# A projection's column blocks in turn: those that VectorE convolves with those that ScalarE copies out

## The chip, the core and the metric

The program runs on one core of one Trainium2 chip. The core has five engines that each work through a list of instructions in order: TensorE (matrix products, PE in the profile), VectorE (DVE), ScalarE (ACT), GpSimd (POOL) and SyncE (SP, which here only starts transfers). Sixteen DMA engines move data between the chip's memory and the core's SBUF. TensorE writes its results into PSUM, in banks, from which VectorE or ScalarE must fetch them. The metric is the device time of one execution in microseconds (us).

## What is computed

One layer of a hybrid decoder, for a prompt of 1,024 tokens and for 8 single new tokens. One input projection feeds three parallel branches; their results are gated, joined and projected back.

```python
h = rms_norm(x) * (1 + scale[:, None]) + shift[:, None]
proj = jnp.dot(h, w['in'])
q_a, k_a, v_a, xbc, dt_raw, qkv_c, beta_raw, a_raw, z = jnp.split(proj, idx, axis=-1)
...
o_a = diff_attention(...)            # q_a, k_a, v_a; the 8 tokens also read a paged cache of 4,096 positions
xbc = jax.nn.silu(causal_conv(xbc) + conv_b)     # Mamba-2 branch, 1,024 columns
qkv = jax.nn.silu(causal_conv(qkv_c))            # gated DeltaNet branch, 3 x 4 heads x 128 columns
... each branch * jax.nn.silu(z)                 # 3 x 512 columns
out = jnp.dot(jnp.concatenate([o_a, o_b, o_c], axis=-1), w['out'])
x = x + gate[:, None] * out
```

## The kernel before, in words

**The projection.** Its columns are done in 44 blocks of 128: 4 of q, 4 of k, 4 of v, 8 of x (the Mamba columns), 12 of z (the gates) and 12 of the DeltaNet branch, three (q, k, v) for each of its heads 0 to 3. `proj_fm` takes the blocks in the order of the list `groups`. A block is three chunks of 344 tokens. A chunk is 24 matmuls (line 458: 8 pieces of the depth, times three products of a split fp32: `whi`*`hh`, `whi`*`hl`, `wlo`*`hh`) into one PSUM bank. The banks come from the ring `pj`, which has three, so a chunk can start only when the chunk three before it has been fetched. After its matmuls a chunk's `sink` runs. A v or z block is fetched by ScalarE, one copy a chunk (lines 600 and 996). An x or DeltaNet block needs a causal convolution over four tokens, which VectorE computes straight out of PSUM: one multiplication (line 969) and three multiply-adds (helper line 167) a chunk, then a copy of the last tokens (line 976, `tail`).

**Silu.** After its third chunk a convolved or z block waits in the list `late_silu`. `silu_flush` gives the list to ScalarE: one activation each, then a load of the table that exp and ln need (line 186), then each block's store to memory. In the kernel before, the list is flushed after three blocks of a DeltaNet head and after two blocks of x or z. ScalarE loads a table (1.28 us) whenever the next function is not in the loaded one; helper line 155 stands for its activations.

**What runs beside.** `drive` interleaves several generators by their costs while the program is written; the framework's scheduler then fixes one order for each engine. Beside the last 33 blocks run: the DeltaNet heads (`gdn_head`, one after another; each needs its three blocks, transposes and scales them, then inverts small triangles by 31 steps on VectorE, tile `U`, with two trips through memory whose transfers ScalarE starts: lines 1129 and 1132 before the steps, 1149 and 1152 after them), the attention of the 8 tokens over the cache (`sample_attention`: a page pair comes in by SP's queue, GpSimd multiplies it, line 840, VectorE reduces it, line 841; after each token's softmax, tile `wz`, TensorE multiplies the value pages, line 896), the weights of the coming blocks (`w_load` on ScalarE's queue, split by ScalarE, tile `whi`, and GpSimd, line 201), and `ssd_sample`, the Mamba step of the 8 tokens (tiles `sst` and `stm` on GpSimd and VectorE). It runs in four quarters, and needs every x block's `tail` (through `conv_sample`) and the z blocks 4 to 7.

**The parts.** `CUTS` splits the 33 blocks into parts. Each part drives its blocks with a share of the heads' and of the pages' work; `ssd_sample` is given to the part that begins after block 18. When the projection ends, the rest (attention of the prompt, the last head, the Mamba scan, the output projection) follows.

The order of the last 33 blocks before is: four v, head 1's three, x 0 to 3, head 2's three, x 4 to 7, twelve z, head 3's three. So from the fifth to the eighteenth VectorE fetches every chunk (called the conv run below), and in the twelve z blocks ScalarE does (the z run).

## Time and profile before

| | us |
|---|---|
| median of 3 runs | 1283.29 |
| lowest and highest of them | 1282.94, 1291.61 |
| the profiled execution | 1288.69 |
| its span, first to last instruction | 1287.0 |
| PE busy in it | 1140.1 (89%) |
| DVE busy | 853.7 (66%) |
| ACT busy | 470.8 (37%) |
| POOL busy | 584.1 (45%) |

The profile comes from one execution, which took 5.4 us more than the median; 1.7 us of it lie outside the span. Busy times count each engine by itself; engines work at the same time, so they don't add up.

### The profile page before, as it was taken

The numbers are of one execution on the slowest core, as the hardware profiler recorded it, in microseconds if no ns is written. First come the engines' busy times: TensorE is split into PE (matmuls) and PEld (weight loads), VectorE is DVE, ScalarE is ACT, GpSimd is POOL, SyncE is SP. The second block draws the span as 40 slices with busy tenths as digits, with TensorE's granted clock in tenths as the row PEclk, the third lists the DMA queues.
The fourth block names the chain that finished last, engine by engine and source line by source line (L and its number), as shares of the span: only waits on it lengthen the run. The fifth ranks groups of instructions, "written<-read, shape, count | busy, mean of one in ns | idle before, by whom it ended". The sixth has DMA issues, their size and how long they took to land.

```text
span 1287.0 us, 21975 instructions
## 1 busy us (share of the span) xinstructions
PE 1140.1 (89%) x7364; PEld 960.7 (75%) x7365; DVE 853.7 (66%) x1994; ACT 470.8 (37%) x998; POOL 584.1 (45%) x395
## 2 busy tenths in 40 slices
PE   4999999988899778979987799997888999799997
PEld 4789887777669568859765678875657878678876
DVE  6624496549388759955763945789878899664444
ACT  6332223112223322133353133426727758442111
POOL 3757874544564633463754666652013242241100
PEclk9999999999799989998998899998998999899999
DMA  8656865985886932795797599899787473971410
GB/s 300 192 178 223 273 218 184 312 272 152 276 289 201 332 117 66 229 336 161 252 299 209 178 293 316 256 313 272 202 233 199 122 191 110 299 227 49 132 69 34
DMA packets 246449, 275.55 MB, mean 214 GB/s; under 512 B 31905, under 2 KB 163376, under 8 KB 246322
## 3 DMA queue, kind: packets, MB, share of 16 engines
q1 hardware_dynamic: 168082, 214.44, 52.1%
q10 hardware_dynamic: 78256, 59.72, 16.4%
q8 instruction: 58, 0.95, 0.3%
q14 instruction: 53, 0.43, 0.1%
HBM read 231.59 MB, written 42.67 MB: 213 GB/s over the span
## 4 chain that ended last, share of the span: by engine, by line
PE 43%; DVE 21%; DMA 19%; issue 5%; ACT 4%; POOL 4%; SPq 2%; ACTq 1%; DVEq 0%; POOLq 0%
PE b L458 15%; PE b L1831 9%; DVE U L159 4%; DMA kt<-in_cache_k_dram 4%; DMA w<-in_w_in_dram 3%; DVE cy L167 3%; PE pv L896 3%; DVE lg L841 3%; DMA vt<-in_cache_v_dram 2%; POOL kt L840 2%; PE b L745 1%; DMA qh<-qfd 1%; DVE cy L969 1%; DMA Dm<-invd 1%; SPq L823 1%
## 5 line engine op out<-in xcount | busy, mean ns | idle before, releaser
L458 PE MATMUL b<-hh,whi 128*128 128x344 f32 (+1 forms) x2016 | 507.0, 335 | 33.0 <-DVE cy L167 21.7
L458 PEld LDWEIGHTS b<-hh,whi 128*128 128x128 f32 x2016 | 362.4, 196 | 68.7 <-issue 33.4
L840 POOL TENSOR_TENSOR kt<-kt,qb 128x1024 f32<-128x1024 f32 x128 | 305.2, 2392 | 203.5 <-DMA kt<-in_cache_k_dram 156.5
L458 PE MATMUL b<-hh,wlo 128*128 128x344 f32 (+1 forms) x1008 | 332.1, 334 | 1.9 <-POOL wlo L201 1.9
L841 DVE TENSOR_REDUCE lg<-kt 128x16 f32<-128x1024 f32 x128 | 154.7, 1212 | 92.1 <-POOL kt L840 78.1
L458 PEld LDWEIGHTS b<-hh,wlo 128*128 128x128 f32 x1008 | 197.2, 197 | 13.4 <-issue 10.8
L201 POOL TENSOR_TENSOR wlo<-w,whi 128x512 fp32r<-128x512 f32 x86 | 111.3, 1301 | 108.6 <-ACT whi L155 96.3
L1831 PE MATMUL b<-wo,mh 128*128 128x512 f32 (+1 forms) x408 | 122.1, 381 | 0.0
L155 ACT ACTIVATE whi<-w 128x512 fp32r<-128x512 f32 x86 | 53.9, 631 | 154.9 <-PE b L458 104.2
L167 DVE SCALAR_TENSOR_TENSOR cy<-b,vec,cy 128x341 f32<-128x341 f32 (+4 forms) x180 | 98.8, 563 | 1.4
L896 PE MATMUL pv<-vt,wz 128*32 128x512 f32 x512 | 80.4, 651 | 18.6 <-DMA vt<-in_cache_v_dram 9.0
L1831 PEld LDWEIGHTS b<-wo,mh 128*128 128x128 f32 x408 | 74.9, 189 | 14.1
L1831 PE MATMUL b<-wo,ml 128*128 128x512 f32 (+1 forms) x204 | 77.2, 379 | 0.0
L1799 POOL TENSOR_TENSOR ml<-zt,mh 128x512 fp32r<-128x512 f32 x16 | 22.4, 1404 | 104.1 <-ACT mh L1798 89.2
L159 DVE TENSOR_TENSOR U<-U,Dm 128x60 f32<-128x60 f32 (+24 forms) x124 | 44.1, 356 | 18.1 <-DMA Dm<-invd 16.2
L156 ACT ACTIVATE e<-e,nmx 128x128 f32<-128x128 f32 (+7 forms) x64 | 49.0, 767 | 7.8 <-DVE nmx L723 5.6
L155 ACT ACT_TABLE_LOAD x33 | 42.3, 1283 | 22.6 <-DMA qh<-qfd 4.6
L718 PE MATMUL b<-kTh,qh 128*128 128x128 f32 (+3 forms) x96 | 40.4, 423 | 9.0 <-DVE mx L721 6.6
L159 DVE TENSOR_TENSOR y<-b,gate 128x512 f32<-128x512 f32 (+1 forms) x17 | 11.1, 658 | 53.6 <-PE b L1831 53.6
L1831 PEld LDWEIGHTS b<-wo,ml 128*128 128x128 f32 x204 | 38.4, 188 | 7.3
L721 DVE CUSTOM_DVE_ANT_0 e<-b,bt 128x512 f32<-128x512 f32 (+3 forms) x64 | 37.0, 581 | 9.9 <-PE b L736 5.8
L159 DVE TENSOR_TENSOR U<-U 128x60 f32<-128x60 f32 (+24 forms) x124 | 39.8, 321 | 2.2
(531 smaller groups left out, 2014.5 us busy)
## 6 DMA issues: line engine op xcount, KB each, us to landing
kt<-in_cache_k_dram SPq DMA_DIRECT2D x256, 256.0 KB
vt<-in_cache_v_dram SPq DMA_DIRECT2D x256, 256.0 KB
w<-in_w_in_dram ACTq DMA_DIRECT2D x82, 256.0 KB
zfd<-zf ACTq DMA_DIRECT2D x12, 512.0 KB
wo<-in_w_out_dram SPq DMA_DIRECT2D x12, 512.0 KB
om<-mixd SPq DMA_DIRECT2D x24, 256.0 KB
xt<-in_x_prompt_dram SPq DMA_DIRECT2D x8, 512.0 KB
hx<-in_w_ada_dram SPq DMA_DIRECT2D x16, 256.0 KB
```

The source lines that it names most:

```text
L155: return S.activation(out, in_, func, bias=bias, scale=scale)
L156: return S.activation(out, in_, func, bias=bias, scale=scale, accum_out=accum)
L159: return V.tensor_tensor(out=out, in0=a, in1=b, op=op)
L167: return V.scalar_tensor_tensor(out=out, in0=a, scalar=s, in1=b, op0=op0, op1=op1)
L201: G.tensor_tensor(out=lo, in0=w32, in1=hi.bitcast(F32), op=ALU.subtract)
L458: TE.matmul(ps[:, 0:N], a, b[k][:, sl], start=(i == 0), stop=(i == 23))
L718: TE.matmul(ps[:, 0:b - a], qh[:, m, ts], kT[m][:, a:b], start=True, stop=False)
L721: V.tensor_tensor_reduce(out=e[m][:, a:b], in0=ps[:, 0:b - a], in1=bias, scale=1.0, scalar=-3.0e38, op0=ALU.add, op1=ALU.max, accum_out=mx ...
L840: G.tensor_tensor(out=kt, in0=kt, in1=bm(qb, 2), op=ALU.mult)
L841: V.tensor_reduce(out=lg[:, 2 * g:2 * g + 2, :], in_=kt.rearrange("p j (a d) -> p j a d", d=64), axis=AX.X, op=ALU.add)
L896: mm = TE.matmul(pv[32 * r:32 * r + 32, :], wz[:, 2 * g + j, :], vt[:, j, :], start=(b == 0 and g < 2), stop=(b == NS - 1 and g >= 14 and ...
L1831: TE.matmul(ps[c], m[a][:, kt % 4, :], w[kt][:, c[0]:c[1]], start=(kt == KT[0] and i == 0), stop=(kt == KT[-1] and i == 2))
```

## The change

The last 33 blocks come in another order. `mixed_items` puts a block that ScalarE copies (v or z) ahead of each block that VectorE convolves, as far as there are enough: v, x0, v, x1, v, g1, v, g1, g1, z, x2, z, x3, z, g2, z, g2, z, g2, z, x4, z, x5, z, x6, z, x7, z, g3, z, g3, z, g3 (g1 is a block of head 1). Three blocks wait for a silu flush instead of two; a head's third block still flushes at once. The parts are cut after block 27 too, since the last x block is the 27th now and not the 18th: `conv_sample` stands after block 27, and `ssd_sample` is given half to blocks 28 to 30 and half to 31 to 33.

```diff
--- before.py
+++ after.py
@@ -35,7 +35,7 @@
 SF = [.05,.80]
 OB = 50
 GF = .77
-CUTS = (9, 18, 30, 33)
+CUTS = (9, 18, 27, 30, 33)
 E_XQ = "svsvsssss"
 SMIX = 3
 SOUT = 1
@@ -975,7 +975,7 @@
             if n == 2:
                 V.tensor_copy(tail[:, tj, :], ps[:, o + m - 3:o + m + NS])
                 late_silu.append((y, silu_bias, done))
-                if flush:
+                if flush or len(late_silu) >= 3:
                     silu_flush()
 
         return (c0, sink, 3)
@@ -996,7 +996,7 @@
             S.copy(cur[0][:, n * CH:(n + 1) * CH], ps)
             if n == 2:
                 late_silu.append((cur[0], 0.0, done))
-                if j % 2:
+                if len(late_silu) >= 3:
                     silu_flush()
 
         return (CZ + j * P, sink, 0)
@@ -1584,16 +1584,28 @@
         def done(y):
             S.dma_start(out=yxd[i], in_=y)
 
-        return conv_item(CX + i * P, 16, 8, i, i, done, i % 2 == 1, vec[:, 48 + i:49 + i])
+        return conv_item(CX + i * P, 16, 8, i, i, done, False, vec[:, 48 + i:49 + i])
+
+    def mixed_items():
+
+        vs, xs, zs = ([f(i) for i in r] for f, r in (
+            (v_item, range(4)), (x_item, range(8)), (z_item, (4, 5, 6, 7, 0, 1, 2, 3, 8, 9, 10, 11))))
+        g = {h: [g_item(h, j) for j in range(3)] for h in (1, 2, 3)}
+        order = []
+        for a, b in ((vs, xs[0:2]), (vs, g[1]), (zs, xs[2:4]), (zs, g[2]), (zs, xs[4:8]), (zs, g[3])):
+            n = len(b)
+            for c in b:
+                if a:
+                    order.append(a.pop(0))
+                order.append(c)
+        assert not vs
+        return order + zs
 
     groups = [
         [q_item(h) for h in range(4)],
         [k_item(h) for h in range(4)],
         [g_item(0, j) for j in range(3)],
-        [v_item(h) for h in range(4)] + [g_item(1, j) for j in range(3)]
-        + [x_item(i) for i in range(4)] + [g_item(2, j) for j in range(3)]
-        + [x_item(i) for i in range(4, 8)] + [z_item(j) for j in (4, 5, 6, 7, 0, 1, 2, 3, 8, 9, 10, 11)]
-        + [g_item(3, j) for j in range(3)],
+        mixed_items(),
     ]
     fg = proj_fm([i for g in groups for i in g], lead_w)
 
@@ -1703,12 +1715,15 @@
         more = []
         if n0 == 0:
             more.append((ada_gate(), 6.0))
-        if n0 == 18:
-            more.append((ssd_sample(cs_out["ssm"]), 9.0))
+        if n0 == 27:
+            one_step = ssd_sample(cs_out["ssm"])
+            more.append((take(one_step, 4.9), 5.0))
+        if n0 == 30:
+            more.append((one_step, 4.0))
         drive((take(fg, 10.5 * (n1 - n0) - (0.1 if n1 < 33 else -9)), 10.5 * (n1 - n0)), (tb, GF * f * B_ALL), ps, *more)
         if n1 == 9:
             sample_v()
-        if n1 == 18:
+        if n1 == 27:
             cs_out["ssm"] = conv_sample(state_ssm_conv, 0, 8, 16, 48)
         n0 = n1
     run(fg)
```

On ScalarE, where head 1 begins: the rows from the fetch of its sums of squares (`ssr`) over its scales (`lnr`) and transposed keys (`kN`) to its factors (`f`). Before, the rows were:

```order
L1053 COPY ssr_4663<-b_4658 128x512
L155 ACTIVATE whi_4909<-w_654_4795 128x512
L155 ACTIVATE whi_5075<-w_686_5041 128x512
L155 ACTIVATE lnr_4765<-ssq_4608 128x16
L1072 COPY kN_4671<-b_4673 128x512
L1072 COPY kN_4671<-b_4739 128x512
L194 DMA w_687_5043<-in_w_in_dram 128x4x128
L194 DMA w_703_5220<-in_w_in_dram 128x4x128
L155 ACTIVATE f_645_4775<-rl_4768 128x16
```

Now the same stretch of head 1 on ScalarE reads:

```order
L1053 COPY ssr_4653<-b_4648 128x512
L1072 COPY kN_4661<-b_4663 128x512
L194 DMA w_703_5204<-in_w_in_dram 128x4x128
L155 ACT_TABLE_LOAD
L155 ACTIVATE lnr_4750<-ssq_4598 128x16
L1072 COPY kN_4661<-b_4724 128x512
L996 COPY zf_4807<-b_4782 128x344
L996 COPY zf_4807<-b_4862 128x344
L996 COPY zf_4807<-b_4953 128x344
L155 ACT_TABLE_LOAD
L155 ACTIVATE f_645_4760<-rl_4753 128x16
```

Where no block was fetched by ScalarE, all three chunks of a z block (`zf`) now stand behind `lnr` and both `kN` copies.

On ScalarE a little later, from the first trip of head 1's triangles through memory: out (`invd<-LT`) and back (`Dm<-invd`). Before, the rows were:

```order
L1129 DMA invd<-LT_4791 32x8x32 x4
L194 DMA w_704_5222<-in_w_in_dram 128x4x128
L155 ACTIVATE whi_5254<-w_703_5220 128x512
L1132 DMA Dm_5013<-invd 32x1024 x4
L194 DMA w_728_5431<-in_w_in_dram 128x4x128
L155 ACT_TABLE_LOAD
L155 ACTIVATE cy_5070<-cy_5070 128x1024
```

Now the same trip on ScalarE reads:

```order
L1129 DMA invd<-LT_4776 32x8x32 x4
L194 DMA w_704_5206<-in_w_in_dram 128x4x128
L155 ACTIVATE whi_5235<-w_703_5204 128x512
L1132 DMA Dm_4997<-invd 32x1024 x4
L194 DMA w_728_5401<-in_w_in_dram 128x4x128
L155 ACT_TABLE_LOAD
L155 ACTIVATE cy_5054<-cy_5054,vec 128x1024
L1585 DMA yxd<-cy_5054 128x1024
L996 COPY zf_5233<-b_5208 128x344
L996 COPY zf_5233<-b_5286 128x344
```

Behind the trip stood the silu of a block of head 2; now a silu of an x block stands there and behind that the chunks of the next z block.

On GpSimd, a quarter of the tokens' Mamba step (`sst`, `stm`) among the pages (`kt`) and weights (`wlo`). Before, the second quarter's rows were:

```order
L875 MEMSET wz 128x32x4
L1410 TENSOR_TENSOR sst_7242<-sst_7242,sexp_6375 128x512 x2
L164 TENSOR_TENSOR stm_7246<-sbc_7244,sxdt_6377 128x256
L164 TENSOR_TENSOR stm_7251<-sbc_7244,sxdt_6377 128x256
L164 TENSOR_TENSOR stm_7257<-sst_7242,sbc_7244 128x256
L164 TENSOR_TENSOR stm_7261<-sst_7242,sbc_7244 128x256
L840 TENSOR_TENSOR kt_7578<-kt_7578,qb_7575 128x1024
L840 TENSOR_TENSOR kt_7650<-kt_7650,qb_7575 128x1024
```

Now the end of the first quarter and the second one on GpSimd read:

```order
L164 TENSOR_TENSOR stm_8313<-sbc_8311,sxdt_8222 128x256
L164 TENSOR_TENSOR stm_8318<-sbc_8311,sxdt_8222 128x256
L1410 TENSOR_TENSOR sst_8571<-sst_8571,sexp_8220 128x512 x2
L164 TENSOR_TENSOR stm_8324<-sst_8309,sbc_8311 128x256
L164 TENSOR_TENSOR stm_8328<-sst_8309,sbc_8311 128x256
L164 TENSOR_TENSOR stm_8575<-sbc_8573,sxdt_8222 128x256
L164 TENSOR_TENSOR stm_8580<-sbc_8573,sxdt_8222 128x256
L164 TENSOR_TENSOR stm_8586<-sst_8571,sbc_8573 128x256
L164 TENSOR_TENSOR stm_8590<-sst_8571,sbc_8573 128x256
L676 MEMSET bt_8763 128x256
L676 MEMSET bt_8766 128x256
L840 TENSOR_TENSOR kt_8632<-kt_8632,qb_8629 128x1024
```

Before, a page product stood behind every quarter; now the first two quarters stand together, and the pages behind both.

## Rows read from the trace of the kernel before

**Rows 1.** The page's first part: busy us, share of the span, instructions.

```profile
PE 1140.1 (89%) x7364; PEld 960.7 (75%) x7365; DVE 853.7 (66%) x1994; ACT 470.8 (37%) x998; POOL 584.1 (45%) x395
```

**Rows 2.** Busy time of each engine in stretches, then granted clock, DMA share, GB/s.

```profile
282.00:579.00 297.00, 256.02 (x1697) 212.25 (x1696) 221.73 (x449) 79.23 (x129) 154.56 (x84) 0.91 0.67 219
579.00:823.00 244.00, 213.76 (x1379) 186.15 (x1380) 146.90 (x263) 86.72 (x147) 140.97 (x93) 0.93 0.79 248
...
867.00:1287.00 420.00, 377.16 (x2304) 306.85 (x2297) 293.08 (x906) 200.84 (x536) 97.19 (x81) 0.96 0.58 165
...
750.00:850.00 100.00, 95.50 (x693) 82.84 (x694) 57.82 (x92) 38.78 (x65) 66.45 (x41) 0.98 0.92 296
```

**Rows 3.** Tiles of a convolved and a z block: ns min/median/max, first and last start.

```profile
L167 DVE SCALAR_TENSOR_TENSOR cy<-b,vec,cy x180: 545/562/577, 164.2 to 873.8; 128x344 f32<-128x344 f32 x60, 128x336 f32<-128x336 f32 x60, 128x341 f32<-128x341 f32 x20, 128x342 f32<-128x342 f32 x20
...
L969 DVE TENSOR_SCALAR cy<-b,vec x60: 546/565/577, 163.6 to 867.4; 128x344 f32<-128x344 f32 x40, 128x336 f32<-128x336 f32 x20
...
L996 ACT COPY zf<-b x36: 425/446/480, 585.1 to 821.4; 128x344 f32<-128x344 f32 x36
```

**Rows 4.** TensorE's waits: us in total, times, longest.

```profile
PE b L458 <- DVE cy L167: 21.7, 9, 8.2
```

**Rows 5.** TensorE in order of time, conv run: start, us, what, idle before it.

```profile
301.15 0.55 PE L458 MATMUL b<-hh,whi 128*128 128x344 f32 x2 [1.05 <-DVE cy L167]
...
454.10 0.94 PE L458 MATMUL b<-hh,whi 128*128 128x344 f32 x2 [8.25 <-DVE cy L167]
...
482.42 0.94 PE L458 MATMUL b<-hh,whi 128*128 128x344 f32 x2 [5.53 <-DVE cy L167]
...
512.81 0.55 PE L458 MATMUL b<-hh,whi 128*128 128x344 f32 x2 [2.39 <-DVE cy L167]
...
540.46 0.56 PE L458 MATMUL b<-hh,whi 128*128 128x344 f32 x2 [2.17 <-DVE cy L167]
```

**Rows 6.** TensorE in order of time, behind the longest of these waits.

```profile
455.13 0.78 PE L458 MATMUL b<-hh,whi 128*128 128x344 f32 x2
...
459.43 0.70 PE L458 MATMUL b<-hh,whi 128*128 128x344 f32 x2
...
462.14 0.48 PE L458 MATMUL b<-hh,whi 128*128 128x348 f32 x2
...
463.56 0.47 PE L458 MATMUL b<-hh,whi 128*128 128x348 f32 x2
```

**Rows 7.** VectorE in order of time, ahead of the longest wait.

```profile
437.19 1.22 DVE L841 TENSOR_REDUCE lg<-kt 128x16 f32<-128x1024 f32 x1 [2.50 <-POOL kt L840]
...
442.14 1.52 DVE L969 TENSOR_SCALAR cy<-b,vec 128x344 f32<-128x344 f32 x3
```

**Rows 8.** TensorE in order of time, z run: waits at head 2 and at the tokens' softmax.

```profile
627.32 3.52 PE L896 MATMUL pv<-vt,wz 128*32 128x512 f32 x16 [2.65 <-DVE wz L159]
...
650.47 3.48 PE L1051 MATMUL b<-sq,ones 128*32 128x512 f32 x8 [3.45 <-ACT sq L155]
...
690.24 0.94 PE L458 MATMUL b<-hh,whi 128*128 128x344 f32 x2 [6.76 <-ACT zf L996]
...
735.77 1.38 PE L896 MATMUL pv<-vt,wz 128*32 128x512 f32 x8 [4.57 <-DVE wz L159]
```

**Rows 9.** ScalarE: its waits (two rows), and a table load in order of time.

```profile
ACT cy L155 <- DVE cy L167: 53.4, 14, 6.8
...
ACT zf L996 <- DMA invd<-U: 15.8, 1, 15.8
...
402.90 1.28 ACT L186 ACT_TABLE_LOAD   x1
...
404.19 0.37 ACT L155 ACTIVATE oC<-b,f 128x128 f32<-128x128 f32 x1
```

**Rows 10.** VectorE in order of time: the tokens' Mamba step ahead of `wz`.

```profile
619.61 2.69 DVE L159 TENSOR_TENSOR sst<-sst,stm 128x512 f32<-128x512 f32 x1
...
734.76 0.75 DVE L164 TENSOR_TENSOR stm<-sbc,sxdt 128x256 f32<-128x256 f32 x2
```

## Prediction

> **What bounds the kernel now.** I read the engines' shares first. TensorE is busy 89% of the span, VectorE 66%, ScalarE 37% [rows 1]. So a gain has to come out of TensorE's other 11%, or out of stretches in which it is busy at half rate; work taken from VectorE or ScalarE alone is worth nothing. Next I cut the span into stages. The change touches the last 33 of 44 column blocks. The two long stages are the conv run (282 to 579 us, fourteen blocks that VectorE fetches) and the z run (579 to 823 us, twelve blocks that ScalarE fetches) [rows 2]. In the conv run TensorE is not busy for 297.0 - 256.0 = 41.0 us, 2.9 a block; in the z run for 244.0 - 213.8 = 30.2 us, 2.5 a block. The reader should see how close these are: the run without any convolution stalls nearly as much, although VectorE is busy 75% in the first and 60% in the second. The 420 us behind the projection keep their work and are taken as unchanged.
>
> Then I asked who releases TensorE. Only 21.7 us of its waits, nine of them, end with a convolution [rows 4]. Five lie in blocks that the change moves: 1.05, 8.25, 5.53, 2.39 and 2.17, together 19.4 us [rows 5]; the rest belongs to head 0's blocks, which stay. The longest is instructive. VectorE works in order; ahead of it stand head 0's last scaling, head 1's first steps and the reductions of cache pages, one of which waits 2.50 us for its page, and only at 442.14 do the first operations of all three chunks of one block follow each other [rows 7]. VectorE was late because a head changed, and the convolutions queued behind that.
>
> **Part 1: VectorE gets two blocks of time for one convolution.** Nothing is removed: a block still has twelve operations of some 0.56 us [rows 3], 6.7 us on VectorE against 1.3 us (three copies of 0.446) on ScalarE, and the two runs together keep VectorE busy for (221.7 + 146.9) / 541 = 68% of their time [rows 2]. What changes is what follows a convolved block: with three banks, TensorE runs two chunks further, then needs the oldest bank; until now VectorE had to free it while the next convolution was arriving too. The three short waits, which stand in runs of convolutions with no head change, should go: 1.05 + 2.39 + 2.17 = 5.6 us. Bounds: 0 if VectorE is as late in the mixture, 5.6 if not. I take 5.6, since VectorE's share there falls from 75% towards 68%.
>
> **Part 2: the head change.** The rows of ScalarE show that head 1 now begins beside a z block whose three fetches stand together behind the head's scales and keys. That is how head 2 begins today, in the z run; there TensorE waits 3.45 us [rows 8] where it waited 8.25 [rows 5]. The nearest row for the new place is thus 3.45, a gain of 4.8 us; bounds 0 and 8.25. Behind the 8.25 us TensorE ran slow: from 455.13 to 459.43 fifteen matmuls took 4.30 us, 0.287 each, where from 462.14 nine took 1.42 us, 0.158 each [rows 6]; that is its granted clock at 1.2 instead of 2.4 GHz after an idle stretch. The slow part lasts from 454.10 to 459.43, 5.33 us, of which 5.33 * (1 - 0.158 / 0.287) = 2.4 us are lost. With the shorter wait I count them as gained (bounds 0 and 2.4).
>
> **Part 3: the triangles' trip through memory.** ScalarE starts these transfers, and in its list the next fetch stands behind them. In the conv run no fetch stood there, and what TensorE waited for beside head 1's trip was a convolution, 5.53 us [rows 5]. In the z run head 2's trip holds the z fetches, and TensorE waits 6.76 us for `zf` [rows 8]. In the new order a z block's fetches follow head 1's trip too. So 5.53 us go and 6.76 come: a loss of 1.2 us (bounds: a loss of 6.8, a gain of 5.5). Queued behind the waiting ScalarE are the weights' splits and the silus; TensorE is who waits for the first.
>
> **Part 4: the tokens' Mamba step.** It moves from beside blocks 19 to 30 to beside 28 to 33. Two waits of TensorE for the softmax weights in the z run, 2.65 and 4.57 us [rows 8], have an operation of this step shortly ahead of `wz` on VectorE, of 2.69 and 0.75 us [rows 10]. It leaves that place and convolutions come. I count half of 7.2, 3.6 us. Its new place is the end of the z run, where VectorE is idle 42 of 100 us [rows 2], which covers it. Without that cover (its first two quarters stand together on GpSimd now, and SP's page loads stand behind their stores) the pages come late. Bounds: a gain of 7.2 and, by the one row of a wait beside a quarter, the 6.76 us at 690, a loss of that size for one quarter more.
>
> **Part 5: the flush of three.** It should save table loads, but ScalarE's order holds 50 before and 52 now, because the silus of one flush become ready at different times and other functions get between them. A load takes 1.28 us and the next activation starts where it ends, 402.90 + 1.28 and 404.19 [rows 9]: 2.6 us more on an engine that is 37% busy, beside TensorE's work. I count nothing. The Trainium skill ("ScalarE: Activation LUTs", What ACT_TABLE_LOAD costs) adds some 1.38 us of drain to each load of 1.283 us, which would make it 5.3 us; the trace agrees with the load but shows no such gap behind this one.
>
> **The sum.** 5.6 + 4.8 + 2.4 - 1.2 + 3.6 = 15.2 us. Against the profiled execution, 1288.69 - 15.2 = 1273.5; that execution lies 5.4 us above the median, so against the median 1283.29 - 15.2 = **1268** us, 1.2% faster. A change of less than about 1% can't be told from none here.
>
> **Rivals.** *More than that goes.* All five waits (19.4), the half rate (2.4) and both waits for `wz` (7.2): 29.0 us, 1254. For it: VectorE and ScalarE fetch in turn, so neither falls behind for long. Against: 30.2 us of idling in the z run without one convolution [rows 2].
>
> *The waits only change their name.* VectorE's order is full at every head whichever block it fetches, so part 2 and its clock bring nothing, and neither does part 4: 5.6 - 1.2 = 4.4 us, 1279. If only the idle time per block evens out, fourteen blocks fall from 2.9 to 2.5, 5.7 us: 1278. For it: the two runs' idle times.
>
> *Slower: ScalarE's list.* A z fetch now often stands behind the silu of a convolved block, and that waits for VectorE. ScalarE has 14 such waits today, 53.4 us in all, 3.8 each and 6.8 at most [rows 9]; nobody wants it then. Seventeen convolved blocks lie in the mixture. If half of their waits, eight, reach TensorE, that costs 8 * 3.8 = 30.5 us against a gain of 15.2: 1299. It decides where ScalarE's wait is longer than TensorE's cover, two chunks of 24 matmuls of 0.158, 7.6 us. Against it: none of the 14 is longer. For it: a wait of 15.8 us has been there for the trip back [rows 9], and the two can follow each other. The Trainium skill ("PSUM — Partial Sum Buffer", Engine vs sequencer instructions) says that ScalarE's and VectorE's queues are strictly first in, first out. By that rule fetches wait behind silus here, and the 15.8 us agree with it.
>
> **How the numbers follow.** Forecast (1260 to 1274) 0.40, more of it (1245 to 1260) 0.20, names changed (1274 to 1291) 0.26, slower (1294 to 1305) 0.14. Two thirds of the forecast lie more than 1% below the median, under 1270.5: faster 0.20 + 0.27 = 0.47, same 0.39, slower 0.14. The range 1249 to 1291 leaves out the slower case and a part of the best.
>
> **What would show it.** In the profile after, TensorE's waits for `cy` should fall from 21.7 to under 8 us, with head 0's two left; the wait at head 1's start should name ScalarE or a sum of squares, at 3 to 4 us; a wait for `zf` should stand at both head 1's and head 2's trip. Table loads should be 52. Wrong would be: waits for `cy` above 12 us (VectorE still late), waits for `zf` or `vT` above 25 us (the slower rival), or waits for `vt`, `wz` or `wlo` at the end of the projection above 10 us (part 4). If the projection's last matmul comes some 15 us earlier but the end doesn't, the stage behind it was not as independent as I took it to be.

## The result, and the profile after

The changed kernel takes 1297.03 us (median of 20 runs, 1286.4 to 1306.61) against 1285.66 us for the kernel before on the same chips: ratio 1.0086, interval 1.0064 to 1.0108. It is slower by 0.9%, where 1.2% faster was forecast.

The profiled execution took 1291.34 us and is the fourth fastest of the twenty; that of before (1288.69) lies above its median. So the two profiles differ by 2.65 us only, and the medians by 11.4: the profiles show why nothing was gained, and the other 8.7 us of the medians they can't show. Over the twenty runs time and granted clock go against each other: the three fastest were granted 0.954 to 0.956, the six slowest 0.937 to 0.947.

The page's first part, after. Against [rows 1] nothing stands out; TensorE is busy 7.6 us longer with the same work (7,365 records of matmuls where there were 7,364).

```profile
PE 1147.7 (89%) x7365; PEld 961.4 (75%) x7365; DVE 851.6 (66%) x1994; ACT 474.0 (37%) x1000; POOL 585.1 (45%) x395
```

What happened is seen when the span is cut by milestones of the work instead of by time: from 205 us up to the start of the projection's last matmul, then to the first transpose of the output stage (L1815 before, L1830 after), then to the end. Stretches of after (columns as in rows 2):

```profile
205.00:842.90 637.90, 579.20 (x3764) 487.07 (x3763) 424.87 (x832) 198.63 (x328) 346.50 (x202) 0.94 0.76 245
842.90:1119.70 276.80, 231.22 (x1549) 181.12 (x1547) 219.51 (x700) 158.19 (x455) 74.11 (x66) 0.92 0.72 194
1119.70:1289.60 169.90, 159.23 (x768) 129.69 (x768) 83.33 (x219) 41.62 (x80) 32.99 (x21) 0.97 0.34 112
```

The same three stretches of before:

```profile
205.00:865.00 660.00, 582.16 (x3781) 487.81 (x3779) 439.26 (x848) 193.89 (x323) 353.31 (x207) 0.93 0.75 241
865.00:1119.60 254.60, 219.81 (x1540) 177.40 (x1539) 212.11 (x687) 160.40 (x460) 65.59 (x61) 0.96 0.75 202
1119.60:1287.00 167.40, 158.19 (x768) 129.76 (x768) 82.62 (x219) 41.65 (x80) 33.60 (x21) 0.97 0.34 112
```

The projection got 22.1 us shorter (660.0 to 637.9), more than the 15.2 forecast; 19.1 of it is idle time of TensorE (77.8 to 58.7). The stage behind it, with head 3, attention and the Mamba scan, got 22.2 us longer (254.6 to 276.8). Both profiles reach the output stage at the same time, 1119.6 and 1119.7; the output stage itself took 2.5 us longer (167.4 to 169.9), and that is the difference of the two profiles. The 22.2 us are 10.8 us more idle time of TensorE (34.8 to 45.6) and 11.4 us more busy time. A little of the busy time is work that moved: eight more matmuls of a value page (line 896) start behind the projection, 88 instead of 80, and those of that line take 12.88 us there instead of 11.42. The granted clock tells where most of the rest comes from. It had two levels in these traces, full and half (2.4 and 1.2 GHz), so a mean of 0.92 instead of 0.96 means half rate for 2 * 0.08 * 276.8 = 44 us instead of 2 * 0.04 * 254.6 = 20. The means are rounded; the clock's own records in the trace add up to 42 and 21 us. Some 21 us more at half rate cost up to 10.

TensorE's waits of after, in us, times, longest:

```profile
PE b L458 <- DVE cy L167: 19.7, 8, 5.8
PE b L856 <- DVE sdg L855: 8.2, 3, 3.6
...
PE b L1051 <- ACT sq L155: 6.7, 4, 2.5
...
PE b L1069 <- DVE ssq L1058: 5.0, 1, 5.0
...
PE pv L896 <- DMA vt<-in_cache_v_dram: 3.6, 3, 1.6
...
PE b L458 <- POOL wlo L201: 3.4, 2, 2.4
...
PE pv L896 <- DVE wz L159: 2.3, 1, 2.3
```

These are waits of the whole execution. Three of those that gave way, as they stood before:

```profile
PE pv L896 <- DMA vt<-in_cache_v_dram: 9.0, 7, 2.5
PE pv L896 <- DVE wz L159: 7.9, 3, 4.6
PE b L458 <- ACT zf L996: 7.2, 2, 6.8
```

The waits for `cy` stay: 19.7 us where [rows 4] have 21.7. In order of time, after:

```profile
443.50 1.11 PE L1069 MATMUL b<-ident,cy 128*128 128x128 f32 x4 [4.96 <-DVE ssq L1058]
...
474.04 0.94 PE L458 MATMUL b<-hh,whi 128*128 128x344 f32 x2 [5.83 <-DVE cy L167]
...
662.60 0.94 PE L458 MATMUL b<-hh,whi 128*128 128x344 f32 x2 [4.25 <-DVE cy L167]
...
779.54 0.94 PE L458 MATMUL b<-hh,whi 128*128 128x344 f32 x2 [3.59 <-DVE cy L167]
```

The convolutions now lie everywhere, and so do the waits for them: beside head 1's trip through memory, where the 5.53 us of [rows 5] stood, but also beside head 2's trip and at the end. At head 1's start a wait for `ssq` stands where the 8.25 us stood.

VectorE at the end of the projection shows where the tokens' Mamba step (`stm`, `sst`, `syS`) went:

```profile
829.73 1.18 DVE L164 TENSOR_TENSOR stm<-sbc,sxdt 128x256 f32<-128x256 f32 x2 [1.83 <-DMA sbc<-bcd]
...
831.44 2.33 DVE L159 TENSOR_TENSOR rsq<-rsq,sm 128x8 f32<-128x8 f32 x1
...
842.67 0.56 DVE L969 TENSOR_SCALAR cy<-b,vec 128x344 f32<-128x344 f32 x1
...
845.92 2.77 DVE L159 TENSOR_TENSOR sst<-sst,stm 128x512 f32<-128x512 f32 x1
...
856.52 0.67 DVE L1419 TENSOR_REDUCE syS<-stm 128x4 f32<-128x512 f32 x1
...
859.32 0.16 DVE L976 COPY tail<-b 128x11 f32<-128x11 f32 x1
```

Its second half runs from 829.7 to 857.2 in front of and between the convolutions of head 3's last block, of which the last ends at 859.4, 16.5 us behind the projection's last matmul (874.4 and 865.0 before: 9.4). TensorE stands still or runs slowly meanwhile. Stretches of after, from the projection's end, and the first such stretch of before:

```profile
842.00:858.00 16.00, 9.01 (x32) 2.67 (x30) 15.96 (x24) 3.10 (x5) 8.29 (x6) 0.79 0.86 230
858.00:874.00 16.00, 11.38 (x44) 7.68 (x44) 11.54 (x52) 9.64 (x28) 4.72 (x2) 0.57 1.11 296
...
865.00:881.00 16.00, 9.24 (x44) 5.99 (x43) 12.84 (x31) 10.51 (x18) 4.40 (x3) 0.75 1.10 270
```

In the first VectorE is busy all the time and TensorE 9 of 16 us, in the second the granted clock is 0.57. That is a part of the loss: when attention's first score starts, 16.8 of the 22.1 us are left (875.7 before, 858.9 after), and when head 3's first state product starts (line 1218), 6.1:

```profile
1026.21 0.38 PE L1218 MATMUL b<-St,kb 128*128 128x128 f32 x2
...
1020.07 0.38 PE L1218 MATMUL b<-St,kb 128*128 128x128 f32 x2
```

The last six go in one place. From head 3's second state product to its third (1038.7 to 1046.4 before, 1032.6 to 1046.2 after) TensorE has nearly the same work, 43 and 42 records. After, it stands idle for 1.85 us there and then runs at half rate for 10.2 us:

```profile
1038.70:1046.40 7.70, 7.57 (x43) 5.41 (x43) 7.12 (x28) 3.02 (x9) 3.74 (x5) 1.00 0.75 201
...
1032.60:1046.20 13.60, 11.72 (x42) 8.77 (x43) 9.20 (x32) 3.44 (x10) 6.27 (x6) 0.65 0.49 141
...
1036.69 0.69 PE L718 MATMUL b<-kTh,qh 128*128 128x384 f32 x1 [1.85 <-DVE mx L721]
```

The first stretch is before's, the second and the wait are after's. From there on head 3's state products start within about a microsecond of each other in the two profiles.

### The profile page after: what moved, and what is told of

It reads as the page before. It is cut to its first block, busy times and chain, and to the rows that moved or that the text cites. A ratio compares the mean times of both kernels' runs of the same rounds, so it can differ in the third digit from the quotient of the medians.

```text
span 1289.6 us, 21969 instructions
## 1 busy us (share of the span) xinstructions
PE 1147.7 (89%) x7365; PEld 961.4 (75%) x7365; DVE 851.6 (66%) x1994; ACT 474.0 (37%) x1000; POOL 585.1 (45%) x395
## 4 chain that ended last, share of the span: by engine, by line
PE 48%; DVE 19%; DMA 16%; issue 6%; ACT 4%; POOL 3%; SPq 2%; ACTq 1%; DVEq 0%; POOLq 0%
PE b L458 20%; PE b L1846 9%; DVE U L159 4%; DMA kt<-in_cache_k_dram 3%; PE pv L896 3%; DMA vt<-in_cache_v_dram 2%; DVE lg L841 2%; DVE cy L167 2%; DMA w<-in_w_in_dram 1%; PE b L745 1%; POOL kt L840 1%; DMA ql<-qfd 1%; DMA sbc<-bcd 1%; DVE e L721 1%; DMA Dm<-invd 1%
## 5 line engine op out<-in xcount | busy, mean ns | idle before, releaser
L458 PE MATMUL b<-hh,whi 128*128 128x344 f32 (+1 forms) x2016 | 505.4, 334 | 21.3 <-DVE cy L167 19.7
L896 PE MATMUL pv<-vt,wz 128*32 128x512 f32 x512 | 77.0, 620 | 8.4 <-DMA vt<-in_cache_v_dram 3.6
L745 PE MATMUL b<-vh,wT 128*128 128x128 f32 x288 | 43.6, 298 | 4.2 <-ACT oA L155 3.0
L745 PEld LDWEIGHTS b<-vh,wT 128*128 128x128 f32 x288 | 39.0, 207 | 9.8 <-ACT oA L155 4.2
```

The source lines that it names most:

```text
L458: TE.matmul(ps[:, 0:N], a, b[k][:, sl], start=(i == 0), stop=(i == 23))
L745: TE.matmul(po[:, 0:P], wTs[j // 4][:, j % 4, :], vh[:, j, :], start=(j == 0), stop=(j == i))
L896: mm = TE.matmul(pv[32 * r:32 * r + 32, :], wz[:, 2 * g + j, :], vt[:, j, :], start=(b == 0 and g < 2), stop=(b == NS - 1 and g >= 14 and ...
```

## The experiments

Each was timed in five rounds. The scheduler fixes every engine's order by its own simulated times, so every edit gives a new list for all engines, behind the edit too. The theories: **A**, the tokens' step in its new place costs what the mixture wins. **B**, the stage behind the projection does not follow the projection's end. **C**, any new list moves the time by up to 1%. **D**, the flush of three delays whatever needs the third silu. **F** (formed late), the stage loses at its start, which no projection block covers.

All results in one table: ratio to before with its interval; from each profile the time of the projection's last matmul, the length of the stage from there to the output stage's first transpose, TensorE's idle time in that stage (its length less the busy time) and its mean granted clock. Times in us. The ratio comes from all runs of a kernel; the other columns come from one profiled execution each, which took between 9.0 us less and 5.1 us more than its kernel's median, so a few us of a stage's length can be chance.

| kernel | ratio | last matmul | stage | idle | clock |
|---|---|---|---|---|---|
| before | 1 | 865.0 | 254.6 | 34.8 | 0.96 |
| after | 1.0086 [1.0064, 1.0108] | 842.9 | 276.8 | 45.6 | 0.92 |
| e1 before's order, late step | 1.0031 [0.9994, 1.0067] | 858.4 | 260.7 | 38.1 | 0.95 |
| e2 mixture, no step | 0.9876 [0.9842, 0.9909] | 839.0 | 264.3 | 38.0 | 0.94 |
| e3 before's order, no step | 1.0086 [1.0053, 1.0118] | 857.2 | 265.0 | 36.1 | 0.92 |
| e4 before's order, flush of three | 1.0024 [0.9984, 1.0065] | 858.0 | 256.4 | 31.8 | 0.93 |
| e5 mixture, step behind the pages | 1.0268 [1.0230, 1.0307] | 830.5 | 320.5 | 72.7 | 0.84 |
| e6 mixture, x and step early | 1.0054 [1.0019, 1.0089] | 845.1 | 266.1 | 39.3 | 0.94 |
| e7 before's order, other z order | 1.0036 [0.9996, 1.0076] | 859.2 | 252.7 | 33.0 | 0.96 |
| e8 mixture, flush of two | 0.9975 [0.9942, 1.0008] | 838.8 | 267.0 | 39.8 | 0.92 |
| e9 e8 without the step | 0.9967 [0.9933, 1.0002] | 830.5 | 281.6 | 45.4 | 0.90 |
| e10 e6 with flush of two | 0.9961 [0.9927, 0.9996] | 843.2 | 267.9 | 33.2 | 0.91 |
| e11 mixture, flush of one | 1.0011 [0.9976, 1.0046] | 833.0 | 284.8 | 45.5 | 0.88 |
| e12 mixture, other z order | 1.0108 [1.0061, 1.0156] | 841.7 | 283.1 | 44.2 | 0.89 |
| e13 before's order, short z | 1.0188 [1.0135, 1.0241] | 859.5 | 274.3 | 42.4 | 0.91 |
| e14 mixture, short z | 1.0100 [1.0064, 1.0137] | 841.0 | 290.8 | 58.2 | 0.90 |
| e15 before, no low part of q | 1.0172 [1.0107, 1.0237] | 862.7 | 275.9 | 52.3 | 0.88 |
| e16 before, no sum of the softmaxes | 1.0171 [1.0119, 1.0223] | 855.4 | 274.8 | 43.1 | 0.90 |
| e17 before's order, head 3 first | 1.0316 [1.0272, 1.0360] | 883.5 | 268.9 | 50.6 | 0.91 |
| e18 e10 with head 3 first | 1.0116 [1.0072, 1.0161] | 857.4 | 269.3 | 49.4 | 0.91 |

### The parts alone: e1 to e4

e1 gives the kernel before the late step, and nothing else:

```diff
-CUTS = (9, 18, 30, 33)
+CUTS = (9, 18, 27, 30, 33)
...
-        if n0 == 18:
-            more.append((ssd_sample(cs_out["ssm"]), 9.0))
+        if n0 == 27:
+            one_step = ssd_sample(cs_out["ssm"])
+            more.append((take(one_step, 4.9), 5.0))
+        if n0 == 30:
+            more.append((one_step, 4.0))
...
-        if n1 == 18:
+        if n1 == 27:
```

> The order of blocks and the flushes are those of before; only the tokens' Mamba step and the tokens' convolution ahead of it move to the end, as in the changed kernel. Theory A (the late step costs what the mixture wins: its 29 us on VectorE, 830 to 859, now lie in front of head 3's convolutions): slower than before by 8 to 15 us, ratio 1.006 to 1.012, with head 3's last convolution more than 14 us behind the projection's last matmul, where it was 9.4. Theory B (the stage behind the projection sets the end by itself, whatever stands ahead of it): ratio 0.997 to 1.003. Theory C (any new list moves the time by some us): anything within 1%, with no such delay at head 3.

e2 (in the changed kernel) and e3 (in that of before) take the step's four quarters out:

```diff
         for q in range(4):
-            st = unit([P, 2, 4, P], n="sst")
...
             yield 2.0
+        V.memset(yS, 0.0)
```

> The changed kernel without the four quarters of the tokens' Mamba step: their states are not loaded, updated or stored, and their sums are zeros. Theory A: against the kernel before without them (next run) faster by 10 to 20 us, since the 22 us by which the projection ends earlier are kept. Theory B: within 5 us of it, the lead is used up between 870 and 1050 us as it is with the step.

> The kernel before without the four quarters of the tokens' Mamba step: their states are not loaded, updated or stored, and their sums are zeros. The pair to the run above. By the prediction's part 4 TensorE's two waits for wz of 2.65 and 4.57 us should shrink and the run be 3 to 8 us faster than before (ratio 0.994 to 0.998). If the step's place there costs nothing, 0.998 to 1.001.

e4 flushes three silus at a time in before's order:

```diff
-                if flush:
+                if flush or len(late_silu) >= 3:
...
-                if j % 2:
+                if len(late_silu) >= 3:
...
-        return conv_item(CX + i * P, 16, 8, i, i, done, i % 2 == 1, vec[:, 48 + i:49 + i])
+        return conv_item(CX + i * P, 16, 8, i, i, done, False, vec[:, 48 + i:49 + i])
```

> The order of before; only the silus are flushed three blocks at a time. By the prediction's part 5 and by theories A and B: nothing, ratio 0.997 to 1.003. A theory D (the silu of one in three blocks now comes a block or two later, and what needs it starts late): slower by 5 us or more, 1.004 and up.

Measured: e1 1290.92, e2 1270.16, e3 1295.73, e4 1287.43 us beside 1285.08 for before. In e1 the last convolution ends 19.9 us behind the last matmul, so the delay that A names is real; its price of 5.8 us is less than the 8 to 15 of A, and the interval holds 1. Leaving the step out of the changed kernel gave 26.9 us, which speaks for A; against its pair e3 it is even 25.6 us, above what A expected. Between these two the projection's lead of 18.2 us arrives whole: their stages last 264.3 and 265.0 us. But e3, with less work than before, is slower than before by 10.7 us, where both expectations had it even or faster. Its projection ends 7.8 us earlier and its stage lasts 10.4 us longer. No theory of work explains that; B and C leave room for it. e4 says nothing certain: by its interval 0.2% faster to 0.6% slower.

### Other places, and the flush: e5 to e8

e5 puts the step's quarters behind the cache pages, e6 brings the x blocks and the step forward, e7 changes one line of before and e8 two of after:

```diff
e5
-            more.append((take(one_step, 4.9), 5.0))
-        if n0 == 30:
-            more.append((one_step, 4.0))
+            more.append((take(one_step, 0.9), 1.0))
...
-        yield from ssd_sample_out()
...
-           (chain(smp, sample_done(), w_out_load(KB, kvp)), (1 - sum(SF)) * S_ALL * SMW)]
+           (chain(smp, one_step, ssd_sample_out(), sample_done(), w_out_load(KB, kvp)), (1 - sum(SF)) * S_ALL * SMW + 9.0)]
e6
-CUTS = (9, 18, 27, 30, 33)
+CUTS = (9, 18, 21, 30, 33)
...
+        for c in "vxvxvgvgg" "xxzgzgxgx" "xzxzzzzzzzgzgzg":
+            order.append({"v": vs, "x": xs, "z": zs, "g": g[1] or g[2] or g[3]}[c].pop(0))
...
+        if n0 == 21:
+            more.append((ssd_sample(cs_out["ssm"]), 9.0))
...
e7
-        + [x_item(i) for i in range(4, 8)] + [z_item(j) for j in (4, 5, 6, 7, 0, 1, 2, 3, 8, 9, 10, 11)]
+        + [x_item(i) for i in range(4, 8)] + [z_item(j) for j in (4, 5, 6, 7, 8, 9, 10, 11, 0, 1, 2, 3)]
e8
-                if flush or len(late_silu) >= 3:
+                if flush or len(late_silu) >= 2:
...
-                if len(late_silu) >= 3:
+                if len(late_silu) >= 2:
```

> The changed kernel with the four quarters of the tokens' Mamba step behind the cache pages, in the stage behind the projection, and nothing left out. Theory A (the step in its new place costs what the mixture wins): most of the 27 us that leaving it out gave come back, 1270 to 1282 us, ratio 0.985 to 0.997 to the kernel before; head 3 begins within 10 us of the projection's last matmul. Theory B' (the stage behind the projection is full, and its 9 us of VectorE cost what they are, wherever they are put): 1290 to 1300.

> Blocks still in turn, but the x blocks 2 to 7 come earlier (v x v x v g v g g, x x z g z g x g x, x z x, then z with head 3's at the end), so that the tokens' Mamba step can stand beside blocks 21 to 30. Theory A: the step is done before head 3, ratio 0.985 to 0.997. If the mixture alone makes it slower (the prediction's rival with ScalarE's list): 1.005 and up. Theory C (any new list moves the time by up to 1% either way): nothing can be said of the direction.

> The kernel before with z blocks 8 to 11 fetched before z blocks 0 to 3: the same work in the same kinds of places, only other columns of the weight. It measures what a new list by itself does. Theories A and B: ratio 0.997 to 1.003. Theory C: 0.4 to 1.0% either way.

> The changed kernel with silus flushed two blocks at a time. By the prediction's part 5: the time of the changed kernel, ratio to before 1.005 to 1.011. Theory D (the flush of three delays what needs the third silu): below 1.004.

Measured: 1318.92, 1289.31, 1286.71 and 1281.93 us beside 1283.31. e5 misses both expectations by far. Stretches of e5 in the stage:

```profile
980.00:1000.00 20.00, 12.33 (x46) 7.85 (x45) 15.34 (x53) 6.33 (x21) 7.65 (x9) 0.67 0.61 147
1000.00:1020.00 20.00, 7.13 (x64) 5.24 (x64) 12.17 (x23) 1.85 (x5) 9.43 (x11) 0.50 0.47 131
```

With the step among attention's and head 3's operations TensorE waits, its longest wait in the stage, 9.2 us, being for the step's result, and the clock falls to half. In this list the stage can't take the step. e6 has the step done by 789 us and is still slower than before, so the late place is not all of it. The control e7 comes out 0.4% slower, by its interval nothing to 0.8%. e8 is the surprise: with two silus at a time the mixture is 1.1% faster than with three, which the prediction priced at nothing.

### Do the costs add? e9 to e12

e9 is e8 with e2's edit, e10 is e6 with e8's, e11 flushes every block at once, e12 is the changed kernel with e7's edit.

> The changed kernel with silus two at a time and without the four quarters of the tokens' Mamba step (states not loaded, updated or stored, sums zero). Left out beside flushes of three, the step gave 26.9 us; the flush of two beside the step gave 15.1. If the two are separate costs that add (theories A and D together): 1297 - 27 - 15 = 1255 us, ratio 0.975 to 0.982. If both only draw another list, which falls anywhere in a band (theory C): 1265 to 1285, ratio 0.985 to 1.0.

> The mixture with x blocks 2 to 7 early and the step beside blocks 21 to 30, silus two at a time; nothing left out. If the costs add (A and D): 1289 - 15 = 1274 us, ratio 0.990 to 0.995, better than the late step with flushes of two (0.9975). Theory C: anywhere from 0.993 to 1.007.

> The changed kernel with each block's silu given at once, so more table loads. Theory D (the wait for the third silu is the cost): as good as two or better but for the loads, ratio 0.993 to 1.001. Theory C: anything from 0.99 to 1.012.

> The changed kernel with z blocks 8 to 11 ahead of z blocks 0 to 3: the same kinds of blocks in the same places. It is the control for the changed kernel. Theories A and D: 1.005 to 1.011, as the changed kernel. Theory C: away from 1.0086 by 0.5% or more either way.

Measured: 1283.47, 1283.39, 1289.81 and 1299.30 us beside 1287.83. The costs do not add. Without the step the flush of two is slower than that of three (0.9967 against 0.9876), beside it faster, with the step late (0.9975 against 1.0086) as with it early (0.9961 against 1.0054). With flushes of two the late step costs nothing that can be measured (e8 against e9). So A and D hold for one list each, not as prices. Yet e12 repeats the changed kernel's 1.0086 with 1.0108: a control that keeps the kinds of blocks keeps the time. C is too strong too: it is not any edit that moves the time by 1%.

In the projection alone the flush shows plainly: its last matmul comes at 833.0, 838.8 and 842.9 us with one, two and three silus at a time. With one the stage then takes 284.8 us.

### What sets the stage behind? e13 to e18

e13 (before) and e14 (after) shorten z blocks 8 to 11, e15 and e16 (both in the kernel before) relieve TensorE and VectorE in the stage:

```diff
e13, e14
-                    for a, b in ((hi, hh), (hi, hl), (lo, hh)):
-                        TE.matmul(ps[:, 0:N], a, b[k][:, sl], start=(i == 0), stop=(i == 23))
+                    for a, b in ((hi, hh), (hi, hl), (lo, hh))[:1 if c0 >= CZ + 8 * P else 3]:
+                        TE.matmul(ps[:, 0:N], a, b[k][:, sl], start=(i == 0), stop=(k == 7 and (b is hh and a is lo or c0 >= CZ + 8 * P)))
e15
-                    TE.matmul(ps[:, 0:b - a], qh[:, m, ts], kT[m][:, a:b], start=True, stop=False)
-                    TE.matmul(ps[:, 0:b - a], ql[:, m, ts], kT[m][:, a:b], start=False, stop=True)
+                    TE.matmul(ps[:, 0:b - a], qh[:, m, ts], kT[m][:, a:b], start=True, stop=True)
e16
-            stt(e[0], e[1], rz[:, 1:2], e[0], ALU.mult, ALU.add)
```

> The kernel before, but z blocks 8 to 11 are multiplied with the weights' high part by the high part alone: 192 of the projection's matmuls are left out, 192 * 0.158 = 30 us of TensorE, all ahead of head 3. Theory B (the stage behind the projection gives back little of what the projection wins; in thirteen profiles the end moves by 0.2 us for each us of the projection's last matmul): 2 to 12 us faster, ratio 0.990 to 0.998, though the projection's last matmul comes 25 to 30 us earlier. If the stage follows the projection, as the prediction took it: 25 to 30 us faster, 0.976 to 0.981.

> The changed kernel with the same 192 matmuls left out. Theory B: 2 to 12 us faster than the changed kernel, ratio to before 0.999 to 1.007. If the stage follows the projection: 25 to 30 us faster than the changed kernel, 0.985 to 0.989.

> The kernel before, but attention's scores are computed without the low part of the queries: 96 matmuls (33.9 us of TensorE) of the stage behind the projection are left out. If TensorE's own work is what that stage lasts as long as: 25 to 34 us faster, ratio 0.974 to 0.981. If VectorE's order or the chains of dependent steps set it: under 10 us, above 0.992.

> The kernel before without VectorE's 32 operations that subtract the second softmax from the first (28.7 us of VectorE in the stage behind the projection; attention's second half of heads is left out of the output). If VectorE sets that stage: 20 to 28 us faster, ratio 0.978 to 0.985. If TensorE does: under 8 us, above 0.994.

Measured: 1304.58, 1295.21, 1305.60 and 1301.93 us beside 1284.88. Every expectation failed, though "above 0.992" and "above 0.994" hold by the letter: none had a slower kernel in mind. Less work made the kernel before slower by 1.7 to 1.9%, and the changed one no faster. The stage in e15 (before's stands above, 865.00 to 1119.60):

```profile
862.70:1138.60 275.90, 223.63 (x1445) 175.84 (x1443) 218.01 (x687) 160.69 (x460) 66.17 (x61) 0.88 0.70 187
```

There are 95 matmuls fewer in the records, but TensorE is busy 223.6 us against 219.8, at a clock of 0.88 against 0.96, and idle 52.3 us against 34.8. Its waits for `mx`, the maxima that VectorE takes of the scores, are 12.2 us in sixteen, where they were 6.6 in eight. So the amount of work of TensorE or of VectorE does not by itself set how long that stage lasts; since each edit also brings a new list, what its work alone is worth can't be told. In e13, 30 us less of TensorE's work brought the last matmul forward by 5.5 us only: the mean clock from 205 us to there fell from 0.93 to 0.91, and idle time rose from 77.8 to 97.0 us.

```profile
205.00:859.50 654.50, 557.49 (x3543) 463.86 (x3543) 435.24 (x829) 186.20 (x316) 345.02 (x203) 0.91 0.74 237
```

A part of this may have a plainer reason than B: TensorE waited 5.9 us more for the weights' high parts (`whi`; first before's wait, then e13's). Whether blocks with a third of the matmuls run ahead of their weights was not tried. Part of its stage is work that moved: sixteen value-page matmuls more run behind the projection, 96 instead of 80.

```profile
PE b L458 <- ACT whi L155: 3.0, 1, 3.0
...
PE b L458 <- ACT whi L155: 8.9, 3, 4.7
```

e17 and e18 let projection blocks cover head 3's start:

```diff
e17
-        + [x_item(i) for i in range(4, 8)] + [z_item(j) for j in (4, 5, 6, 7, 0, 1, 2, 3, 8, 9, 10, 11)]
-        + [g_item(3, j) for j in range(3)],
+        + [x_item(i) for i in range(4, 8)] + [z_item(j) for j in (4, 5, 6, 7, 0, 1, 2, 3)]
+        + [g_item(3, j) for j in range(3)] + [z_item(j) for j in (8, 9, 10, 11)],
e18 (against e10)
-        for c in "vxvxvgvgg" "xxzgzgxgx" "xzxzzzzzzzgzgzg":
+        for c in "vxvxvgvgg" "xxzgzgxgx" "xzxzzzzzgzgzgzz":
```

> The kernel before with head 3's three blocks ahead of z blocks 8 to 11, so that head 3's start and attention's first steps have projection blocks of TensorE beside them; nothing left out. Theory F (the stretch from the projection's last matmul to attention's first score, with TensorE idle and then at half clock, is where the stage loses): that stretch falls under 6 us from 10.7, half-clock time behind the projection stays near 21 us, ratio 0.990 to 0.998. Theory C: a new list, ratio 0.997 to 1.012, with more half-clock time than 30 us behind the projection.

> The mixture with x early and silus two at a time (the run of 0.9961), now with head 3's blocks two z blocks before the end. Theory F: the stretch falls under 6 us from 13.0, ratio 0.985 to 0.993. Theory C: 0.990 to 1.006.

Measured: 1324.26 and 1298.09 us beside 1283.84. The stretch from the last matmul to attention's first score does fall to 2.1 us in both, and the kernels are slower by 3.2 and 1.2%, outside what F and C had. F falls as it was written. Why e17 is that slow is open: its last matmul comes 18.5 us later than before's, and its stage is longer although 74 matmuls of head 3 have left it.

### What follows from the table

Take the eight mixtures that leave the projection's matmuls whole, keep head 3 last and don't put the step behind the pages (after, e2, e6, e8 to e12) against the five kernels in before's order (before, e1, e3, e4, e7). The mixtures' last matmul comes at 839.3 us on average, the others' at 859.6. The output stage begins at 1113.2 and at 1117.4. Of 20.3 us that the mixture wins, 4.2 arrive. The ratios, which rest on all runs, say the same: 1.0005 on average against 1.0035, 0.3% or 3.9 us. That is B on average; single lists lie up to 12 us to either side of it, and in the pair e2 and e3 the whole lead arrives. The long stages have both more idle time and a lower clock: among these thirteen the three longest (e9, e11, e12) have 44 to 46 us and 0.88 to 0.90, the three shortest (before, e4, e7) 32 to 35 and 0.93 to 0.96.

The best kernel that leaves nothing out is e10: 0.9961 of before, interval 0.9927 to 0.9996. That is less than 1%, which the prediction took as no difference.

## Why the prediction was wrong

**The step that failed** is the sentence "The 420 us behind the projection keep their work and are taken as unchanged". The time is not kept: the stage between projection and output took 254.6 us before and 276.8 after, and 253 to 291 over all lists but e5's. Nor is the work quite kept. The step's end and eight value-page matmuls slid behind the projection: in the stage VectorE is busy 219.51 us where it was 212.11, and GpSimd 74.11 where it was 65.59. Left out of the mixture, the step gives 12.5 us of the stage back (e2); left out of before's order, it makes the stage 10.4 us longer (e3), so even this is no price that holds in another list. The check written for this case (the last matmul some 15 us earlier and the end not) is what came, with 22.1. It was one of the things that would make the prediction wrong, and it had neither a price nor a chance of its own.

**Part 1** (5.6 us): wrong in place, since waits for `cy` stay at 19.7 us, over the 12 named as wrong. VectorE did not fall behind less often; it is late at head 1, head 2 and the end, a few us each. The gain in the projection came from other waits: those for `vt`, `wz` and `zf` were 24.1 us in all before, over the whole execution; after, the first two are 5.9 and the third has left the list. Those for `sdg`, `sq` and `ssq` took back a part of it. The projection's gain of 22.1 us is thus larger than the 15.2 of the sum and made of other terms; that the two are of a size is luck.

**Part 2** (4.8 + 2.4): right in kind. The wait at head 1's start names a sum of squares, 4.96 us instead of 8.25; it was put at 3.45, so 3.3 of the 4.8 us came. The 2.4 us of the clock did not: behind the shorter wait TensorE ran at half rate for about as long, with a mean granted clock of 0.53 from 443.5 to 450.0, against 0.55 from 454.1 to 460.5 before.

**Part 3** (-1.2): the wait for `zf` at head 1's trip did not come, and the one of 6.76 us at head 2's went; waits for `cy` stand at both, 5.83 and 4.25 us. Together that is 2.2 us less than before, where 1.2 more was forecast.

**Part 4** (+3.6): the waits for `wz` shrank to one of 2.3 us, somewhat more than counted, and e3 bears out their cause: with the step left out of before's order they are 3.2 us in one, where they were 7.9 in three. Its cover was the mistake. VectorE's idle 42 of 100 us [rows 2] belonged to the old order; in the new one convolutions lie there, VectorE is busy 79.72 of 100 us, and the step slid to 857 us:

```profile
750.00:850.00 100.00, 86.94 (x528) 74.23 (x528) 79.72 (x141) 30.93 (x48) 67.47 (x51) 0.93 0.86 266
```

The price named for that, pages that come late, was not the one paid: the late things were head 3's convolutions. In before's order, by itself, the late step costs 0.3%, and the interval includes no change (e1).

**Part 5** (0): 52 table loads, as read from the order. But the number of silus that a flush holds is worth 0.9 to 1.1% beside the step, with the opposite sign without it. How is not shown. With three instead of two the projection's last matmul comes 1.9 to 8.5 us later in the mixtures. With the step late the stage behind adds 9.8 us; with the step early (e6, e10) the two profiled executions took the same time, 1280.3 us, and show nothing of it.

**The rivals.** The slower one gave 1299 us, close to what was measured, by a mechanism that is not there: no wait for `zf` or `vT` of note. So its number says nothing for it. The other two ended faster or even and had the same fault as the forecast.

**What stays open** is what in a list makes the same stage last 253 or 285 us. It isn't the projection's end, one engine's amount of work, the uncovered start or the step's place alone; each was tried, though always together with a new list. Open too are the 8.7 us of the medians that the profiles don't hold. What is shown is only how the time is lost: TensorE waits some 10 us more, in many waits of 1 to 4 us, and runs at half rate for some 20 us more behind them.

## What to carry to other kernels

Where a scheduler writes every engine's order, no stage behind an edit is unchanged: give it a term and a range, and read a control with a neutral edit beside every gain of a per cent (here another order of z blocks moved the time by 0.2 and 0.4%, each uncertain by 0.4 or more). Compare profiles by milestones of the work, since a lead that is won and given back leaves both totals alike. And less work is no gain by itself: of seven kernels here with work left out one was faster than before by over 1%, and five were slower.

## What the runs showed of the hardware

**Idle time costs twice.** The stretches of e15 and e5 above show TensorE granted 0.88 and, over 20 us with 7.13 busy, 0.50; fewer matmuls then took more busy time. I had counted the clock only behind one wait of 8.25 us; in the stage it is about half of the loss (up to 10 of 22.2 us), and the stretch from 1032.6 to 1046.2 above shows one such place: 1.85 us of waiting, then 10.2 us at half rate.

**VectorE can stand still beside GpSimd.** The scaling of 128x8 numbers at 831.44 above took 2.33 us. The same operation before:

```profile
874.36 0.15 DVE L159 TENSOR_TENSOR rsq<-rsq,sm 128x8 f32<-128x8 f32 x1
```

After, it ends with GpSimd's product. GpSimd in order of time:

```profile
831.35 2.41 POOL L840 TENSOR_TENSOR kt<-kt,qb 128x1024 f32<-128x1024 f32 x1
...
845.79 2.35 POOL L840 TENSOR_TENSOR kt<-kt,qb 128x1024 f32<-128x1024 f32 x1
```

831.35 + 2.41 = 833.76 and 831.44 + 2.33 = 833.77; likewise the 2.77 us at 845.92 end 0.55 us behind the product that ran until 848.14, and such an operation with GpSimd idle takes 0.69:

```profile
833.89 0.69 DVE L159 TENSOR_TENSOR sst<-sst,stm 128x512 f32<-128x512 f32 x1
```

The Trainium skill ("SBUF — State Buffer", Who interferes with whom) says that an instruction of VectorE with two inputs in SBUF contends with one of GpSimd that reads SBUF, and that the order of issue decides which of them is held up. These rows agree with it: GpSimd's product started first both times, 0.09 and 0.13 us ahead. The late step put GpSimd's and VectorE's products side by side just where head 3's convolutions were due.
